# Four token tiles of the last chunk accumulated ahead of its last two steps, statistics of six tiles on ScalarE, and all blocks of u ahead of the operand differences

## The chip, the cores and the metric

The kernel runs as one program on one core of a Trainium2 chip. The metric is device time in microseconds (us) from start to end of one execution; the median of three executions is compared.

## The reference

Two blocks are computed one after the other on 1024 tokens (rows) of width 1024, in float32; the first has two layers. What the change touches are the feed-forward parts and the layer norms behind them:

```python
    # first block, each layer: mixer, then
        x = layer_norm(ALPHA * x + gate * y, ln_g[layer, 0], ln_b[layer, 0])
        u = x * (1.0 + scale) + shift
        y = jnp.square(jax.nn.relu(u @ mlp_w1[layer] + mlp_b1[layer])) @ mlp_w2[layer] + mlp_b2[layer]
        x = layer_norm(ALPHA * x + gate * y, ln_g[layer, 1], ln_b[layer, 1])
    # second block: mixer, then
        x = _layernorm(DEEPNORM_ALPHA * x + mix, ln1_g, ln1_b)
        h = _causal_depthwise_conv(x @ w_up, conv_f_w, conv_f_b)
        gate, val = h[..., :D_FF_2], h[..., D_FF_2:]
        ffn = (jax.nn.silu(gate) * val) @ w_down
        x = _layernorm(DEEPNORM_ALPHA * x + ffn, ln2_g, ln2_b)
```

There are three such parts: the MLP of layer 0 (4096 wide, some 470 to 1165 us of the span), the MLP of layer 1 (some 1978 to 2690 us) and the gated FFN of the second block (2816 wide, some 2993 us to the end).

## The kernel before

**Matmuls.** Every float32 operand is split into a high part (a cast on ScalarE, ACT) and a low part (source minus high part, a subtraction on VectorE, DVE), and every product is three TensorE (PE) matmuls: high by high, high by low, low by high. The casts and subtractions of weights are in `ws.split` (L216, L218; tiles `wl`, `wu`), those of the other operands in lines L1339 (`we`), L1446 (`he`) and L577 (`u`). GpSimd is called POOL, SyncE (which issues the loads and stores) SP. Each engine runs its instructions in the order of the program; a wait holds up all that stands behind it on that engine.

**The three stages of a feed-forward part.** `boundary` finishes the stage ahead: for each of 8 token tiles (128 rows) it accumulates the last weight blocks (`last_sums`, 12 matmuls for each half of 512 columns), adds them to the rows (`acc` or `xres`), takes mean and variance (`bn_stats`, L627), works out one over the root (`ln_fin`, a chain of small DVE instructions) and normalises on ACT (L631). Then it transposes the rows into `u` tiles (`u_tile`: 4 transposes on PE, scale and shift on ACT L576, cast on ACT L577, low part on DVE), eight for each half of the tokens, and runs the first three column blocks of the up projection (`fm_mms`, tiles `pss[0]` to `pss[2]`, two halves of some 48 matmuls each). `FmProducts` then does the up projection with seven products in the place of eight for each 2 x 2 block; its operands from `u` are differences of blocks, which `diffs` works out: eight DVE subtractions and four ACT casts into tiles `t`, four times. Its weight operands `we` come from sums of weight blocks (`sf`, `wx`, made on POOL) and are split on ACT and DVE. `TmProducts` does the down projection in chunks, seven steps j = 0 to 6 to a chunk, each with operands `he` from `rh` (loaded) and `rw` (weights and their sums); it splits the operands of the next step during a step, and adds each step's PSUM result (`ps`, or the two smaller buffers `pb`) to `acc` on DVE.

**Where the sum ends.** `second_half` runs `TmProducts` with a function `step` that is called four times in each step; in the last chunk it calls `add_residual` (load of the saved residual rows into `zi`, in an MLP a product with the gate row on POOL, then an addition on DVE) for the four quarters of `acc` and `ws.split` for the eight blocks that remain: four of `h` and four of w2, which a plain product sums at the end (`tail_blocks`, `last_sums`). The remaining splits spread over steps 0 to 6. For an MLP the next `boundary` does those last sums, for the FFN `finish`: for each token tile two halves of 12 matmuls, two additions, `bn_stats`, `rsqrt` (twelve small DVE instructions for a pair of tiles, nine for one) and `scale` (four DVE instructions of 128x512, or ACT and POOL for the halves listed in `_FIN_POOL`), then the store.

**The place of u and differences.** In `boundary` the u tiles of the second half are made during the first half's matmuls in the order of blocks 0, 4, 1, 5, 2, 6, 3, 7, and `diffs` follows every second of them:

```python
                    u_tile(xres, 1, kt, uT, G, B, uf=raw(1, kt))
                    if kt > 3 and ops is not None:
                        diffs([[raws[h, kt - 4 + 4 * a] for a in range(2)] for h in range(2)], ops)
```

Of the kernel before, what the change touches and what calls it, by code (L numbers as in the profile page):

```python
# [12 lines left out]
AF = mybir.ActivationFunctionType  # L13
# [241 lines left out]
def tile_net(ctx: ExitStack, tc: tile.TileContext, x, wts, ada, adag, cols, rows, sfm, rgw, wup, wsp, out):  # L255
# [118 lines left out]
    st = _K()  # L374
    st.direct = {}
    plan = []

# [129 lines left out]

    def last_sums(hs, wsx, t):

# [10 lines left out]
        if t == 0:  # L520
            o = [PSUM()[:, 0:512] for _ in range(2)]
            for dh in range(2):
                mms(o[dh], dh, range(n - 1))
            for dh in range(2):
                mms(o[dh], dh, [n - 1])
                yield o[dh]
        else:
            for dh in range(2):
                o = PSUM()[:, 0:512]
                mms(o, dh, range(n))  # L530
                yield o
# [38 lines left out]
    def u_tile(xz, h, kt, uT, G, B, lo=None, uf=None):  # L570
# [7 lines left out]
        tt(uT[h][:, 1, kt, :], uf, uT[h][:, 0, kt, :].bitcast(F32), SUB, lo)  # L578

    def boundary(hs, wsx, xres, G, B, keys, evacs, spill=None, ops=None):  # L580

# [26 lines left out]
        raws = {}  # L608
        for t in range(8):
            s6 = smt(12, "s6").rearrange("p (a b) -> p a b", b=6)  # L610
            if t == 5:
                alloc_u(uT, 0)
            sums = last_sums(hs, wsx, t)
            for dh in range(2):
                if t >= 5:
                    for _ in range({(5, 0): 2, (6, 0): 2}.get((t, dh), 1)):
# [6 lines left out]
                if t == 0 and dh == 0:  # L623
# [12 lines left out]
            else:  # L636
                z()
            if t == 1 and spill is not None:
                rr[0], rr[1] = T4("gr"), T4("cr")
                xrows(*spill[1:], rr[0], rr[1])  # L640
            if t in (2, 4, 6):
                ws.split(ws.ng + t // 2, lo=pool)
        pss = [PSUM() for _ in range(3)]
# [731 lines left out]
    class TmProducts:  # L1375
# [89 lines left out]

        def run(self, xres, step):
            aa = None
            for g in range(self.n):
# [8 lines left out]
                for t in range(4):  # L1477
# [98 lines left out]
    class Mlp:  # L1576
# [20 lines left out]
        def run(self, uT, jobs=None):  # L1597
# [47 lines left out]
            undefer(9)  # L1645
            return second_half(l, tp, 2 * l + 1, residual_job(ALPHA, f"lng{2 * l}", f"lnb{2 * l}", (f"b2_{l}", 2 * l + 1)))

# [20 lines left out]

    def second_half(l, tp, gate, job):

# [21 lines left out]
        def step(g, t):  # L1692
# [9 lines left out]
        tp.run(xres, step)  # L1702
        add_residual(xres, gate, 1, 0)
        hs, w2 = tail_blocks()
        return hs, w2, xres

# [588 lines left out]
    def ffn(bargs):  # L2295
# [68 lines left out]
        undefer(9)  # L2364
        return second_half(2, tp, None, residual_job(ALPHA2, "ln1g", "ln1b", None))

    def finish(hs, wsx, xres):
# [22 lines left out]
        for t in range(8):  # L2390
# [3 lines left out]
            s6 = smt(12, "s6").rearrange("p (a b) -> p a b", b=6)  # L2394
            for dh, o in enumerate(last_sums(hs, wsx, t)):
                f = slice(dh * 512, (dh + 1) * 512)
                tt(xres[:, t, f], xres[:, t, f], o, ADD)
                dve.bn_stats(out=s6[:, dh, :], in_=xres[:, t, f])
            dve.bn_aggr(out=mv[:, len(group) - 1, :], in_=s6)
            if later and t < 7:  # L2400
# [6 lines left out]
            if t == 6:  # L2407
                scale(*later.pop(0))
        for g in later:
            scale(*g)  # L2410


    with tc.manual_schedule():
# [25 lines left out]
        xres, w2 = st.xres, tail_end()  # L2439
        hs, w2, xres = ffn((w2[4:8], w2[0:4], xres, C("ln1g", 0, 8), C("ln1b", 0, 8), [("up", 0), ("up", 22), ("up", 1)]))  # L2440
        finish(hs, w2, xres)

# [18 lines left out]
```

## Time and profile before

| | us |
|---|---|
| median of three executions | 3713.23 (3707.98 to 3713.67) |
| the profiled execution | 3706.28 |
| its span (first to last instruction) | 3704.4 |
| PE busy | 3515.9, 95% of the span |
| DVE busy | 2663.2, 72% |
| ACT busy | 1469.9, 40% |
| POOL busy | 568.2, 15% |

The profile is of one execution. Its groups of instructions give a count, the mean duration of one and the idle time of the engine ahead of them with what ended it; its timeline gives start and duration of every instruction; its stretches give busy times, the granted clock of PE (PEclk; 1.00 is 2.4 GHz, 0.50 is 1.2 GHz) and DMA. PE is busy for 95% of the span, so that nearly all that can be won or lost lies in the few stretches where PE stands.

### The profile page before, as it was taken

The numbers are of one execution on the slowest core, as the hardware profiler recorded it, in microseconds if no ns is written. First come the engines' busy times: TensorE is split into PE (matmuls) and PEld (weight loads), VectorE is DVE, ScalarE is ACT, GpSimd is POOL, SyncE is SP. The second block draws the span as 40 slices with busy tenths as digits, with TensorE's granted clock in tenths as the row PEclk, the third lists the DMA queues.
The fourth block names the chain that finished last, engine by engine and source line by source line (L and its number), as shares of the span: only waits on it lengthen the run. The fifth ranks groups of instructions, "written<-read, shape, count | busy, mean of one in ns | idle before, by whom it ended". The sixth has DMA issues, their size and how long they took to land. (4 is left out here: it accounts for less than half of the span.)

```text
span 3704.4 us, 43629 instructions
## 1 busy us (share of the span) xinstructions
PE 3515.9 (95%) x17098; PEld 2864.4 (77%) x17098; DVE 2663.2 (72%) x3640; ACT 1469.9 (40%) x1957; POOL 568.2 (15%) x415
## 2 busy tenths in 40 slices
PE   7999899999999999999899999999989999999997
PEld 5877778887877778888787888877768677777765
DVE  5574767868997764454647666798889677877897
ACT  4254353343335442443425334432413354444431
POOL 2002113300022000000202331002200013322002
PEclk9999999999999999999999999999989999999998
DMA  6343235465642222100122445574210323222662
GB/s 228 109 135 122 80 129 190 174 229 199 238 132 93 71 81 81 46 30 30 67 93 104 149 148 213 190 264 137 100 54 29 125 76 110 88 87 104 222 218 91
DMA packets 184160, 469.16 MB, mean 127 GB/s; under 512 B 15601, under 2 KB 20353, under 8 KB 183954
## 3 DMA queue, kind: packets, MB, share of 16 engines
q1 hardware_dynamic: 177378, 446.35, 34.1%
q0 software_dynamic: 6576, 20.03, 1.6%
q8 instruction: 134, 2.20, 0.2%
q14 instruction: 72, 0.59, 0.0%
HBM read 340.99 MB, written 125.32 MB: 126 GB/s over the span
## 5 line engine op out<-in xcount | busy, mean ns | idle before, releaser
L247 PE MATMUL ps<-u,wu 128*128 128x512 f32 x2880 | 755.6, 408 | 13.9 <-ACT u L577 5.3
L247 PEld LDWEIGHTS ps<-u,wu 128*128 128x128 f32 x2880 | 533.0, 192 | 140.1 <-issue 14.0
L247 PE MATMUL ps<-he 128*128 128x512 f32 x2442 | 582.9, 397 | 28.0 <-DVE he L305 21.7
L247 PEld LDWEIGHTS ps<-he 128*128 128x128 f32 x2442 | 460.6, 190 | 144.6 <-DVE he L305 33.0
L247 PE MATMUL ps<-t,we 128*128 128x512 f32 x1728 | 423.5, 393 | 5.4 <-DVE cc L305 5.3
L247 PEld LDWEIGHTS ps<-t,we 128*128 128x128 f32 x1728 | 323.4, 188 | 83.3 <-DVE cc L305 8.8
L247 PE MATMUL pb<-u,we 128*128 128x512 f32 x1152 | 281.9, 393 | 0.0
L247 PE MATMUL ps<-wu,u 128*128 128x256 f32 x1920 | 262.5, 291 | 16.4 <-DVE wu L218 14.3
L247 PEld LDWEIGHTS ps<-wu,u 128*128 128x128 f32 x1920 | 243.0, 193 | 27.4 <-DVE wu L218 15.1
L247 PEld LDWEIGHTS pb<-u,we 128*128 128x128 f32 x1152 | 216.2, 188 | 49.5 <-DVE we L305 0.2
L1446 ACT CAST he<-rw 128x1024 fp32r<-128x1024 f32 (+1 forms) x154 | 132.7, 911 | 240.4 <-DVE rw L305 227.0
L247 PE MATMUL ps<-pw,wu 128*128 128x512 f32 x816 | 211.3, 407 | 14.5 <-DVE xres L308 8.8
L1925 DVE TENSOR_REDUCE mx<-ps 128x1 f32<-128x128 f32 (+7 forms) x128 | 95.6, 755 | 173.5 <-PE ps L247 173.1
L305 DVE TENSOR_TENSOR we<-sf,we 128x512 fp32r<-128x512 f32 x192 | 153.9, 814 | 85.7 <-ACT we L1339 84.7
L305 DVE TENSOR_TENSOR he<-rw,he 128x1024 fp32r<-128x1024 f32 (+1 forms) x154 | 162.6, 1098 | 61.4 <-ACT he L1446 61.2
L1965 ACT ACTIVATE p<-ps 128x1024 f32<-128x1024 f32 (+7 forms) x128 | 82.9, 649 | 304.2 <-PE ps L247 288.4
L247 PEld LDWEIGHTS ps<-pw,wu 128*128 128x128 f32 x816 | 155.0, 194 | 51.5 <-DVE xres L308 9.2
L305 DVE TENSOR_TENSOR he<-rh,he 128x1024 fp32r<-128x1024 f32 (+1 forms) x154 | 165.9, 1079 | 18.6 <-ACT he L1446 18.4
L1446 ACT CAST he<-rh 128x1024 fp32r<-128x1024 f32 (+1 forms) x154 | 136.5, 911 | 88.5 <-DMA rh<-d_h 81.7
L305 DVE TENSOR_TENSOR acc<-acc,ps 128x1024 f32<-128x1024 f32 (+1 forms) x148 | 154.1, 1042 | 17.0 <-PE ps L247 16.6
L305 DVE TENSOR_TENSOR we<-wx,we 128x512 fp32r<-128x512 f32 x144 | 134.3, 934 | 44.5 <-ACT we L1339 44.5
L247 PE MATMUL pb<-he 128*128 128x512 f32 x666 | 158.5, 392 | 0.0
(395 smaller groups left out, 5847.7 us busy)
## 6 DMA issues: line engine op xcount, KB each, us to landing
st<-in_wts_dram SPq DMA_DIRECT2D x108, 512.0 KB, 3.4
rh<-d_h SPq DMA_DIRECT2D x105, 512.0 KB, 5.4
sf<-in_wts_dram SPq DMA_DIRECT2D x96, 512.0 KB, 6.6
d_h<-hx SPq DMA_DIRECT2D x37, 1024.0 KB, 5.1
d_h<-rr SPq DMA_DIRECT2D x111, 256.0 KB, 2.3
sta<-in_ada_dram SPq DMA_DIRECT2D x48, 512.0 KB, 3.6
rw<-in_wts_dram SPq DMA_DIRECT2D x28, 768.0 KB, 6.1
sta<-in_adag_dram SPq DMA_DIRECT2D x32, 512.0 KB, 3.9
```

The lines of the kernel that those rows point to most:

```text
L247: return self.eng.matmul(out=out, lhsT=lhsT, rhs=rhs, **kw)
L305: (eng or dve).tensor_tensor(out=o, in0=a, in1=b, op=op)
L1446: act.copy(d[:, 0, 0:n, :], src)
L1925: dve.tensor_reduce(out=mx[:, t:t + 1], in_=ps[:, 0:n], axis=AX.X, op=ALU.max)
L1965: act.activation(out=p[:, 128 * i:1024], in_=ps[:, 128 * i:1024], func=AF.Exp)
```

## The change

Three things are changed.

1. **Early tiles.** After step j = 4 of the last chunk a new function `mid` is called: it adds the quarter (0,1) of the residual, splits the last two weight blocks (`tail_blocks`) and accumulates and normalises token tiles 0 to 3 (`early_tiles` in an MLP, the first half of `finish`, now a generator, in the FFN), with the small PSUM buffers `pb` (two of them) in the place of `ps` (three). Steps 5 and 6 follow. `boundary` then begins at tile 4 and makes one u tile in each half of tiles 4 to 7.
2. **Statistics.** In `finish` the mean and variance of tiles 0 to 5 come from two ACT instructions with an accumulated output (Copy, then Square with the negative mean as bias), with one small DVE instruction between them; tiles 6 and 7 keep `bn_stats`.
3. **u ahead of differences.** The four calls of `diffs` come after all eight u tiles of the second half: the first within the second half of `pss[0]`, the second behind it, the third behind the first evacuation, the fourth behind the matmuls of `pss[2]`.

```diff
+    def early_tiles(hs, wsx, xres):
+        for t in range(4):
+            s6 = smt(12, "s6").rearrange("p (a b) -> p a b", b=6)
+            for dh, o in enumerate(last_sums(hs, wsx, t, True)):
+                xr = xres[:, t, dh * 512:(dh + 1) * 512]
+                tt(xr, xr, o, ADD)
+                dve.bn_stats(out=s6[:, dh, :], in_=xr)
+            y, nb = ln_fin(s6)
+            act.activation(out=xres[:, t, :], in_=xres[:, t, :], func=AF.Identity, scale=y, bias=nb)
+        st.first = 4
...
-                    if kt > 3 and ops is not None:
-                        diffs([[raws[h, kt - 4 + 4 * a] for a in range(2)] for h in range(2)], ops)
+        def diff(j):
+            if ops is not None:
+                diffs([[raws[h, j + 4 * a] for a in range(2)] for h in range(2)], ops)
+
         for c, _ in enumerate(fm_mms(pss[0], w[0], uT, 1)):
             if c % 2:
                 residual(4 + c // 2)
+            if c == 3:
+                diff(0)
+        diff(1)
         ws.split(ws.ng + 1, True, lo=pool)
         run(fm_mms(pss[1], w[1], uT, 1))
         evacs[0](pss[0])
+        diff(2)
         run(fm_mms(pss[2], w[2], uT, 1))
+        diff(3)
         evacs[1](pss[1])
...
+                if g == self.n - 3:
+                    mid()
...
             if g >= tp.n - 7:
-                if t == 3 and j in (2, 5, 6):
-                    add_residual(xres, gate, *((0, 0), (0, 1), (1, 1))[(2, 5, 6).index(j)])
-                ws.split(min(ws.ng + 8, max(ws.ns, ws.ng + (4 * j + t) // 3)))
+                if (j, t) == (2, 3):
+                    add_residual(xres, gate, 0, 0)
+                elif (j, t) == (6, 0):
+                    add_residual(xres, gate, 1, 1)
+                if j < 5:
+                    ws.split(min(ws.ng + 8, max(ws.ns, ws.ng + (4 * j + t) // 3)))
...
+        def mid():
+            add_residual(xres, gate, 0, 1)
+            r.extend(tail_blocks())
+            early(*r, xres)
+        tp.run(xres, step, mid)
         add_residual(xres, gate, 1, 0)
...
+            else:
+                xr, dev = xres[:, t, :], T4("dev")
+                act.activation(out=dev, in_=xr, func=AF.Copy, scale=1.0 / 1024, accum_out=m[:, 0:1])
+                nm = smt(1, "nm")
+                ts(nm, m[:, 0:1], -1.0 / 32, None, MUL)
+                act.activation(out=dev, in_=xr, func=AF.Square, bias=nm, scale=1.0 / 32, accum_out=m[:, 1:2])
```

DVE's queue in the boundary of layer 0's MLP, before, from the low part of the second pair of u tiles on (`tx`, `ur`, `t`: a set of differences):

```order
L305 TENSOR_TENSOR u_3557<-ur,u_3557 128x512
L305 TENSOR_TENSOR u_3559<-ur,u_3559 128x512
L305 TENSOR_TENSOR tx<-ur 128x512
L305 TENSOR_TENSOR tx<-ur,tx 128x512
L305 TENSOR_TENSOR ur<-ur,tx 128x512
L305 TENSOR_TENSOR ur<-ur 128x512
L305 TENSOR_TENSOR t_3637<-tx,t_3637 128x512 x2
L305 TENSOR_TENSOR t_3638<-ur,t_3638 128x512 x2
L305 TENSOR_TENSOR u_3558<-ur,u_3558 128x512
L305 TENSOR_TENSOR u_3560<-ur,u_3560 128x512
```

And after, on the same engine from the third u tile on:

```order
L305 TENSOR_TENSOR u_3557<-ur,u_3557 128x512
L305 TENSOR_TENSOR u_3559<-ur,u_3559 128x512
L305 TENSOR_TENSOR u_3558<-ur,u_3558 128x512
L305 TENSOR_TENSOR u_3560<-ur,u_3560 128x512
L305 TENSOR_TENSOR u_3558<-ur,u_3558 128x512
L305 TENSOR_TENSOR u_3560<-ur,u_3560 128x512
L305 TENSOR_TENSOR tx<-ur 128x512
L305 TENSOR_TENSOR tx<-ur,tx 128x512
L305 TENSOR_TENSOR ur<-ur,tx 128x512
L305 TENSOR_TENSOR ur<-ur 128x512
L305 TENSOR_TENSOR t_3689<-tx,t_3689 128x512 x2
L305 TENSOR_TENSOR t_3690<-ur,t_3690 128x512 x2
```

The u tiles stand in a row now, and the four sets of differences in a row behind them.

DVE's queue in the last chunk of the FFN, before, from the sum of weights for step 6 on (`rw`); `acc<-acc,pb` is the result of step 4:

```order
L305 TENSOR_TENSOR rw<-rw 128x1536
L305 TENSOR_TENSOR acc<-acc,pb 128x512
L305 TENSOR_TENSOR he<-rw,he 128x1024
L305 TENSOR_TENSOR he<-rw,he 128x512
L305 TENSOR_TENSOR he<-rh,he 128x1024
L305 TENSOR_TENSOR acc<-acc,ps 128x2x512
L218 TENSOR_TENSOR wl<-st,wl 128x1024
L305 TENSOR_TENSOR he<-rh,he 128x512
L305 TENSOR_TENSOR acc<-acc,ps 128x2x512
L305 TENSOR_TENSOR acc<-acc,zi 128x2x512 x2
L218 TENSOR_TENSOR wl<-st,wl 128x1024
```

And after; behind these rows come the rest of tiles 0 to 3 (a `rsqrt` for tiles 0 and 1, the additions of tiles 2 and 3, the `scale` of tile 1, a `rsqrt` for tiles 2 and 3), and only then the four rows of `he`:

```order
L305 TENSOR_TENSOR rw<-rw 128x1536
L305 TENSOR_TENSOR acc<-acc,pb 128x512
L305 TENSOR_TENSOR acc<-acc,zi 128x2x512 x2
L218 TENSOR_TENSOR wl<-st,wl 128x1024 x2
L305 TENSOR_TENSOR acc<-acc,pb 128x512 x2
L312 TENSOR_SCALAR nm<-mvp 128x1
L305 TENSOR_TENSOR acc<-acc,pb 128x512 x2
L312 TENSOR_SCALAR nm<-mvp 128x1
```

The additions of `zi` and the last two splits of w2 stand right behind step 4's result, ahead of the additions of tile 0, and the operands `he` of step 6 stand behind all of tiles 0 to 3. The same holds in the two MLPs.

SP's queue at the end of the program, a piece of the difference:

```order
-L1524 DMA zi<-d_zm 128x2x512 x6
-L2387 DMA out_dram<-acc 128x512 x16
-L2457 UNCONDITIONAL_BRANCH
+L1548 DMA zi<-d_zm 128x2x512 x2
+L2424 DMA out_dram<-acc 128x512 x4
+L1548 DMA zi<-d_zm 128x2x512 x4
+L2424 DMA out_dram<-acc 128x512 x12
+L2506 UNCONDITIONAL_BRANCH
```

The stores of tiles 0 and 1 stand ahead of the last four loads of the residual.

## Rows read from the trace of the kernel before

**Rows 1.** Stretches: us, each engine's busy time (instructions), PEclk, DMA share, GB/s.

```profile
480.00:497.00 17.00, 12.64 (x46) 9.57 (x47) 14.58 (x24) 11.84 (x19) 0.00 (x0) 0.80 0.28 93
1049.90:1165.00 115.10, 102.81 (x461) 81.18 (x460) 95.35 (x169) 43.07 (x54) 32.36 (x20) 0.99 0.24 82
2563.40:2690.00 126.60, 118.58 (x536) 95.77 (x536) 113.13 (x199) 47.75 (x58) 40.28 (x18) 0.99 0.30 104
```

**Rows 2.** Who PE waited for, 470 to 525 us: total us, times, longest.

```profile
PE pb L251 <- ACT ur L576: 4.8, 2, 2.4
PE ps L247 <- ACT u L577: 1.7, 1, 1.7
```

**Rows 3.** DVE's instructions in order of time, 473 to 517 us: start, us.

```profile
475.36 0.69 DVE L305 TENSOR_TENSOR tx<-ur 128x512 f32<-128x512 f32 x1
...
480.63 0.69 DVE L305 TENSOR_TENSOR u<-ur,u 128x512 fp32r<-128x512 f32 x1
481.96 0.69 DVE L305 TENSOR_TENSOR u<-ur,u 128x512 fp32r<-128x512 f32 x1 [0.64 <-ACT u L577]
...
513.24 0.69 DVE L305 TENSOR_TENSOR we<-sf,we 128x512 fp32r<-128x512 f32 x1 [2.36 <-ACT we L1339]
```

**Rows 4.** All engines in order of time, 504 to 530 us.

```profile
501.93 2.47 POOL L218 TENSOR_TENSOR wu<-st,wu 128x1024 fp32r<-128x1024 f32 x1 [41.47 <-ACT wu L216]
...
521.21 2.96 PE L247 MATMUL ps<-u,we 128*128 128x512 f32 x12
```

**Rows 5.** All engines in order of time, 3025 to 3050 us.

```profile
3026.18 2.60 DVE L308 SCALAR_TENSOR_TENSOR rr<-ps,col,rr 128x1023 f32<-128x1023 f32 x2 [0.86 <-ACT rr L2304]
...
3044.45 2.92 PE L247 MATMUL ps<-u,we 128*128 128x512 f32 x12
```

**Rows 6.** All engines in order of time, 1045 to 1072 us.

```profile
1049.90 11.11 PE L247 MATMUL ps<-he 128*128 128x512 f32 x48
...
1053.91 0.68 DVE L305 TENSOR_TENSOR acc<-acc,pb 128x512 f32<-128x512 f32 x1
...
1054.67 2.42 POOL L305 TENSOR_TENSOR acc<-acc,gate 128x1024 f32<-128x1024 f32 x1 [3.96 <-DVE acc L305]
...
1061.65 3.28 POOL L305 TENSOR_TENSOR acc<-acc,gate 128x1024 f32<-128x1024 f32 x1 [4.57 <-DVE acc L305]
...
1062.63 3.39 DVE L305 TENSOR_TENSOR he<-rh,he 128x1024 fp32r<-128x1024 f32 x1
```

**Rows 7.** DMA issues of the whole span: KB each, median us to landing.

```profile
zi<-d_zm SPq DMA_DIRECT2D x24, 512.0 KB, 4.4
```

**Rows 8.** PE in order of time, 2595 to 2605 us.

```profile
2600.02 5.32 PE L247 MATMUL ps<-wl,wu 128*128 128x512 f32 x15 [3.93 <-DVE acc L305]
```

**Rows 9.** All engines in order of time, 2556 to 2584 us.

```profile
2561.54 2.38 DVE L218 TENSOR_TENSOR wl<-st,wl 128x1024 fp32r<-128x1024 f32 x1
...
2563.45 13.08 PE L247 MATMUL ps<-he 128*128 128x512 f32 x56
```

**Rows 10.** All engines in order of time, 3612 to 3640 us.

```profile
3615.88 16.77 PE L247 MATMUL ps<-he 128*128 128x512 f32 x72
...
3617.42 0.68 DVE L305 TENSOR_TENSOR acc<-acc,pb 128x512 f32<-128x512 f32 x1
...
3625.54 2.36 DVE L305 TENSOR_TENSOR acc<-acc,zi 128x1024 f32<-128x1024 f32 x2
```

**Rows 11.** DVE's and ACT's instructions in order of time, 3664 to 3704 us.

```profile
3685.68 0.15 DVE L314 TENSOR_SCALAR lnv<-mvp 128x1 f32<-128x1 f32 x1
...
3690.13 0.74 DVE L308 SCALAR_TENSOR_TENSOR acc<-acc,mvp,orow 128x512 f32<-128x512 f32 x1
...
3693.02 0.21 DVE L314 TENSOR_SCALAR nb<-mvp,lny 128x1 f32<-128x1 f32 x1
```

**Rows 12.** ACT's groups of instructions by line and shape: busy us, mean ns.

```profile
L631 ACT ACTIVATE acc<-acc,nb,lny 128x1024 f32<-128x1024 f32 x16 | 19.9, 1243 | 78.7 <-DVE nb L314 78.7
...
L1081 ACT ACTIVATION_READ_ACCUMULATOR wk<-pb 128x1 f32 x32 | 6.6, 207 | 0.0
```

More of the change, by code (lines that the diff above doesn't have):

```diff
@@ L375, in tile_net @@
     st.direct = {}
+    st.first = 0
     plan = []
@@ L506, in tile_mms, with last_sums @@
         return ps
-    def last_sums(hs, wsx, t):
+    def last_sums(hs, wsx, t, small=False):
         n = len(hs)
@@ L520, in last_sums @@
         if t == 0:
-            o = [PSUM()[:, 0:512] for _ in range(2)]
+            o = [PB() if small else PSUM()[:, 0:512] for _ in range(2)]
             for dh in range(2):
@@ L528, in last_sums @@
             for dh in range(2):
-                o = PSUM()[:, 0:512]
+                o = PB() if small else PSUM()[:, 0:512]
                 mms(o, dh, range(n))
@@ L608, in boundary @@
         raws = {}
-        for t in range(8):
+        first, st.first = st.first, 0
+        ut = 4 if first else 5
+        for t in range(first, 8):
             s6 = smt(12, "s6").rearrange("p (a b) -> p a b", b=6)
-            if t == 5:
+            if t == ut:
                 alloc_u(uT, 0)
@@ L614, in boundary @@
             for dh in range(2):
-                if t >= 5:
-                    for _ in range({(5, 0): 2, (6, 0): 2}.get((t, dh), 1)):
+                if t >= ut:
+                    for _ in range(1 if first else {(5, 0): 2, (6, 0): 2}.get((t, dh), 1)):
                         kt = todo.pop(0)
@@ L622, in boundary @@
                 o = next(sums)
-                if t == 0 and dh == 0:
+                if t == first and dh == 0:
                     flush()
@@ L637, in boundary @@
                 z()
-            if t == 1 and spill is not None:
+            if t == (4 if first else 1) and spill is not None:
                 rr[0], rr[1] = T4("gr"), T4("cr")
                 xrows(*spill[1:], rr[0], rr[1])
-            if t in (2, 4, 6):
-                ws.split(ws.ng + t // 2, lo=pool)
+            if t in ((4, 5, 6) if first else (2, 4, 6)):
+                ws.split(ws.ng + (t - 3 if first else t // 2), lo=pool)
         pss = [PSUM() for _ in range(3)]
@@ L1464, in fetch, with run @@
                 self.weights(c + 1, *((0, 0), (1, 0), (0, 1), (1, 1))[j - 2])
-        def run(self, xres, step):
+        def run(self, xres, step, mid):
             aa = None
@@ L1645, in run @@
             undefer(9)
-            return second_half(l, tp, 2 * l + 1, residual_job(ALPHA, f"lng{2 * l}", f"lnb{2 * l}", (f"b2_{l}", 2 * l + 1)))
+            return second_half(l, tp, 2 * l + 1, residual_job(ALPHA, f"lng{2 * l}", f"lnb{2 * l}", (f"b2_{l}", 2 * l + 1)), early_tiles)
     def begin(tp, i):
@@ L1667, in begin, with second_half @@
             tp.sums(2)
-    def second_half(l, tp, gate, job):
+    def second_half(l, tp, gate, job, early):
         xres = Rows("acc")
@@ L1696, in step @@
             if g >= tp.n - 7:
-                if t == 3 and j in (2, 5, 6):
-                    add_residual(xres, gate, *((0, 0), (0, 1), (1, 1))[(2, 5, 6).index(j)])
-                ws.split(min(ws.ng + 8, max(ws.ns, ws.ng + (4 * j + t) // 3)))
+                if (j, t) == (2, 3):
[4 more added lines that the diff above has]
+                    ws.split(min(ws.ng + 8, max(ws.ns, ws.ng + (4 * j + t) // 3)))
             elif g == tp.n - 8 and t == 3:
                 run(side_work)
-        tp.run(xres, step)
+        r = []
+        def mid():
[3 more added lines that the diff above has]
+        tp.run(xres, step, mid)
         add_residual(xres, gate, 1, 0)
-        hs, w2 = tail_blocks()
-        return hs, w2, xres
+        return r[0], r[1], xres
     def zip_cost(a, b, rate, at_end):
@@ L2364, in ffn, with early_out @@
         undefer(9)
-        return second_half(2, tp, None, residual_job(ALPHA2, "ln1g", "ln1b", None))
+        return second_half(2, tp, None, residual_job(ALPHA2, "ln1g", "ln1b", None), early_out)
+    def early_out(hs, wsx, xres):
+        st.fin = finish(hs, wsx, xres)
+        next(st.fin)
     def finish(hs, wsx, xres):
@@ L2394, in finish @@
             s6 = smt(12, "s6").rearrange("p (a b) -> p a b", b=6)
-            for dh, o in enumerate(last_sums(hs, wsx, t)):
+            m = mv[:, len(group) - 1, :]
+            for dh, o in enumerate(last_sums(hs, wsx, t, t < 4)):
                 f = slice(dh * 512, (dh + 1) * 512)
                 tt(xres[:, t, f], xres[:, t, f], o, ADD)
-                dve.bn_stats(out=s6[:, dh, :], in_=xres[:, t, f])
-            dve.bn_aggr(out=mv[:, len(group) - 1, :], in_=s6)
+                if t > 5:
+                    dve.bn_stats(out=s6[:, dh, :], in_=xres[:, t, f])
+            if t > 5:
+                dve.bn_aggr(out=m, in_=s6)
+            else:
[4 more added lines that the diff above has]
+                act.activation(out=dev, in_=xr, func=AF.Square, bias=nm, scale=1.0 / 32, accum_out=m[:, 1:2])
             if later and t < 7:
@@ L2408, in finish @@
                 scale(*later.pop(0))
+            if t == 3:
+                yield
         for g in later:
@@ L2439, in tile_net @@
         xres, w2 = st.xres, tail_end()
-        hs, w2, xres = ffn((w2[4:8], w2[0:4], xres, C("ln1g", 0, 8), C("ln1b", 0, 8), [("up", 0), ("up", 22), ("up", 1)]))
-        finish(hs, w2, xres)
+        ffn((w2[4:8], w2[0:4], xres, C("ln1g", 0, 8), C("ln1b", 0, 8), [("up", 0), ("up", 22), ("up", 1)]))
+        run(st.fin)
 def kernel(**inputs):
```

## The prediction

> **What bounds the kernel now.** The page says that PE is busy for 95% of the span, so I looked for the stretches that the change touches and, in each, for the time in which PE stands. The stretches come first [rows 1]: in the boundary ahead of layer 0's first product (480 to 497 us) PE is busy for 12.64 of 17.0 us at a granted clock of 0.80; at the end of layer 0's MLP and in the boundary behind it PE idles 115.1 - 102.8 = 12.3 us, in layer 1's 126.6 - 118.6 = 8.0 us, and there DVE is busy for 113 of 126.6 us. So DVE, with PE's clock behind it, is what these boundaries wait for. The second view is who PE waited for [rows 2]: 4.8 + 1.7 us for ACT's parts of u tiles. The third is time order, for what DVE and POOL do at the places of change [rows 3 to 6, 9 to 11]. The sum is made against the profiled execution's 3706.3 us, which lies 6.9 us under the median of 3713.2.
>
> **u ahead of differences (three boundaries).** A set of differences takes DVE 480.63 - 475.36 = 5.3 us, 5.2 without the gap, and the low parts of u wait behind it [rows 3]; that is PE's wait of 6.5 us. Beside it stands the lower clock: at 0.80 over 17 us, some 6.8 us at 1.2 GHz, of which PE worked three quarters and lost half, 2.5 us. Both go: 9.0 us for each boundary, the same pattern standing at all three. What comes late next is the first product's weights `we`, which stand behind all differences on DVE. In an MLP: from 475.4 six more u tiles at the pace of 1.33 us (481.96 - 480.63) end at 483.4; four sets of differences, 20.8, end at 504.2. POOL has its split of 2.47 us [rows 4] and three sums of weights in the same time, together some 6.4 us (the sums taken at half of its split). DVE's two-operand instructions stand still while POOL runs one: an operand of 1.2 us took 3.39 beside a POOL product of 3.28 [rows 6]. So 510.6; four subtractions of `hx` at 0.69, 513.4; casts and splits of `we`, some 2.5, 516. PE would be there at 521.2 - 9.0 = 512.2 [rows 4], and waits 4; behind a wait of 3.9 us PE was seen to take 5.32 us for 15 matmuls [rows 8] that take 3.5 at the pace of 72 in 16.77 [rows 10], so 1.9 us more at the lower clock. Gain 9.0 - 4 - 1.9 = **3 us in each MLP**. In the FFN three convolutions stand in DVE's queue as well, 3 x 2.6 us and a product of 1.2 [rows 5], with no `hx`: by the same walk 3007 + 20.8 + 6.4 + 9.0 + 2 = 3045, against PE at 3044.45 - 9.0 = 3035.4. The wait is 9.8 + 1.9, a **loss of 2.7 us**. Before, the covers were 8 us from `we` (513.24) to PE's use (521.21): the change spends them. Bounds: 9 gained in each if POOL holds nothing up, 3 lost in each if more is held up. Sum taken: -3.3 us.
>
> **Early tiles in layer 0's MLP.** PE reaches tile 0 at 1049.9 [rows 6]. Six matmuls (1.4 us) use the first two w2 blocks; then it needs the third, whose low part now stands on DVE behind the last result of step 4 (1053.91 + 0.68), and two additions of `zi`, which wait for POOL's gate product (1054.67 + 2.42 = 1057.1) [rows 6]. Two additions at 1.2 and one split at 1.2 make 1060.7: PE waits 9 us from 1051.3, and 1.9 us go at the lower clock. Two PSUM buffers in the place of three cost about 1 us more (each half has 2.8 us of PE work, its addition 0.7). What was waiting for that work before, 12.3 us of idle time and perhaps 1 of clock, does not all go: the u tiles and the normalisations of tiles 4 to 7 stay in order. I take half, 6 + 1. Loss 12 - 7 = **5 us** (bounds: all of it goes, 0; none goes, 12). Steps 5 and 6 cover the normalisations of tiles 0 to 3; that is the gain in that half.
>
> **The same in layer 1.** Here the two loads of `zi` share a buffer in the row of the temporaries: the first can issue when the split at 2561.54 is done (2563.9) [rows 9], lands 4.4 us later [rows 7] and is added at 2569.5; the second takes its place, lands at 2573.9 and is added at 2575.1; the split makes 2576.3. PE, at tile 0 from 2563.45 [rows 9], waits from 2564.9: 11.4 us, 1.9 at the lower clock, 1 for the buffers, 14.3 together. Against it half of 8.0 and the 1.9 behind the wait of 3.93 [rows 8]: **loss 8.5 us** (bounds 4 and 15).
>
> **The end.** PE reaches tile 0 at 3615.9, needs the third block at 3617.3 and gets it at 3617.4 + 0.7 + 2.4 + 1.2 = 3621.7 [rows 10]: 4.4 us, 1.9 of clock, 1 of buffers. The other 90 matmuls (21.0) end at 3645.6, step 5 (36 matmuls, 8.4) at 3654. Step 6's operands `he` now stand on DVE behind tiles 0 to 3: last addition 3646.3, ACT's Copy with its accumulator (no such row; by the normalisation's 1.24 and an accumulator read's 0.21 [rows 12], 1.45; bounds 1.0 and 2.0), `scale` of tile 1 (4 x 0.75 [rows 11]), a `rsqrt` of 12 small instructions at 0.15 to 0.21 each [rows 11], 2.4, and three splits of 0.6 to 1.2: 3656.4. PE waits 2.4 us, loses some 1 of clock, ends step 6 at 3665.8 and the second half of tile 5 at 3677.0. From there DVE leads: addition 0.7, Copy 1.45 and the negative mean, `scale` of tile 3 (3), `rsqrt` (2.4): 3685.0; tile 6's additions and `bn_stats`, 3.0; `rsqrt`, 2 to 4.45 (beside POOL 3685.68 to 3690.13 [rows 11]); tile 7's, 3.0; `rsqrt`, 2 to 4.45; `scale` of tile 6, 2.9. The last `nb`, at 3693.02 before [rows 11], comes at 3698 to 3703, and what follows it is unchanged. The statistics moved to ACT take four times 0.7 us off DVE for tiles 4 and 5, but put DVE behind ACT's Copy for 1.45 us a tile. SP's four stores ahead of the last `zi` loads cost nothing: those additions stand behind step 6's operands at 3656. **Loss 7.4 us** (5 to 10).
>
> **Sum.** -3.3 + 5 + 8.5 + 7.4 = 17.6 us slower, 3723.9 against the profiled execution, **3731 us** against the median.
>
> **The rivals.**
>
> *POOL does not hold DVE up at the new places.* Then the MLPs' weights come by 509.6, ahead of PE's 512.2, and each boundary keeps its 9 us; the FFN waits 3.4 + 1.9 and keeps 3.7; the last stretch loses 5, the other two 4 and 8.5: -21.7 + 17.5 = -4.2 us, 3709 us, not slower. It decides at `we`'s readiness before 512.2. Against it stands the operand that took 3.39 in the place of 1.2 us [rows 6]; for it, that POOL may have run its instructions in the u tiles' time, where DVE has gaps of 0.64 us [rows 3]. The Trainium skill (Advanced Engine Details and Errata, VectorE Performance Modes) says that GpSimd and two-port VectorE instructions block each other, and lists no two-port mode for a tensor_tensor; by that rule alone this rival holds, and the trace speaks against it.
>
> *DVE's total decides in the boundaries.* With 113 of 126.6 us busy, PE's wait at tile 0 is only one that it would have had later. Both boundaries come out even, 17.6 - 13.5 = 4.1 us slower, 3717. It decides where DVE's idle time does not grow; against it, DVE itself stands for two loads and POOL's product.
>
> *Both together:* -17.7 us, 3695.
>
> *All at the bad bounds:* 3 lost at each `we`, 9 and 13 in the boundaries, 10 at the end, 9 + 22 + 10 = 41, 3754.
>
> **How the numbers follow.** The forecast has 0.50, the first rival 0.15, the second 0.15, both 0.10, the last 0.10. Of the forecast some lies either side of its 3731 by the halves taken, 3722 to 3742. A measurement of this kernel tells 0.2%, 7.4 us, from no change: faster is under 3705.8, same up to 3720.7. Faster: both rivals together and a third of the first, with part of the halves taken too large, 0.17; same: the rest of the first and nearly all of the second, 0.23; slower: 0.60. The range of 3700 to 3745 leaves out most of the case of both and most of the last, under 2 in 10.
>
> **What would show it.** In the profile after, PE's waits for u should be gone from 480 to 497 us, and a wait for `we` of about 4 us (MLPs) and 10 us (FFN) should stand ahead of the first product; PE should wait 9, 11 and 4 us for `wl` early in tile 0; a wait for `he` should stand ahead of step 6 of the last chunk; and the last `nb` should be reached by way of DVE, not PE. The forecast is wrong if `we` is ready ahead of PE, if the loads of `zi` have landed early so that the splits follow step 4 at once, or if the waits of tiles 4 to 7 vanish altogether.

## The result, and the profile after

| | before | changed |
|---|---|---|
| median, us | 3710.61 (3707.92 to 3713.67, 4 runs) | 3733.14 (3728.49 to 3733.74, 4 runs) |
| ratio to before | | 1.0053, 95% interval 1.004 to 1.0065 |
| span of the profiled execution | 3704.4 | 3726.7 |
| PE busy | 3515.9 | 3518.9 |

The change makes the kernel 0.53% slower, some 22 us; 3731 was forecast. PE does the same work (17098 matmuls in both traces): what is new is waiting, and the lower clock behind it. To see where, the same matmul (by its count from the start; the count stands in the same place of the program outside the reordered stretches) is looked up in both traces. The table gives by how much it starts later in the trace after:

| stretch | on entry | on leaving | change | forecast |
|---|---|---|---|---|
| u and first product, layer 0 (470 to 530 us) | +0.1 | -5.2 | -5.3 | -3 |
| end of layer 0's MLP, boundary (1040 to 1170) | -4.3 | +0.4 | +4.7 | +5 |
| u and first product, layer 1 (1978 to 2040) | +1.5 | -3.9 | -5.4 | -3 |
| end of layer 1's MLP, boundary (2540 to 2692) | -4.9 | +5.1 | +10.0 | +8.5 |
| u and first product, FFN (2990 to 3055) | +4.8 | +5.7 | +0.9 | +2.7 |
| FFN's last steps to the end (3590 on) | +7.9 | +22.3 | +14.4 | +7.4 |

The rest, 3 us, is drift between the stretches. The sum of the six rows is 19.3 us where 17.6 were forecast, so the sum came out well; but the first part won more than forecast, 9.8 us in place of 3.3, and the end lost about twice as much. The last row even hides some of that loss: 2.6 us are won between 3590 us and the place where tile 0 begins (3615.9 before, 3621.2 after, +5.3), in steps that the change leaves as they were. From tile 0 on, which is what the forecast of 7.4 is about, the loss is 17.0 us.

**Ahead of the first products.** Who PE waited for in the trace after, 470 to 530 us and 2985 to 3065 us (total us, times, longest):

```profile
PE ps L247 <- ACT we L1361: 3.4, 1, 3.4
...
PE ps L247 <- ACT we L1361: 9.2, 1, 9.2
```

The waits for u [rows 2] are gone, and those for `we` stand in their place, 4 and 9.8 us in the forecast. The trace after in order of time, 484 to 520 us, shows who held `we` up:

```profile
494.71 2.45 POOL L218 TENSOR_TENSOR wu<-st,wu 128x1024 fp32r<-128x1024 f32 x1 [34.10 <-ACT wu L216]
494.82 2.89 DVE L305 TENSOR_TENSOR tx<-ur 128x512 f32<-128x512 f32 x1
...
499.68 1.62 POOL L305 TENSOR_TENSOR wx<-wx,sf 128x512 f32<-128x512 f32 x1
500.07 1.77 DVE L305 TENSOR_TENSOR ur<-ur 128x512 f32<-128x512 f32 x1
...
508.13 1.15 ACT L1296 CAST t<-ur 128x512 fp32r<-128x512 f32 x2 [0.78 <-DVE ur L305]
...
513.37 0.60 ACT L1361 CAST we<-sf 128x512 fp32r<-128x512 f32 x1
...
514.03 4.79 PE L247 MATMUL ps<-u,we 128*128 128x512 f32 x12 [3.45 <-ACT we L1361]
```

The subtraction `tx<-ur`, 0.69 us in [rows 3], takes 2.89 while POOL's split takes 2.45, and `ur<-ur` 1.77 beside POOL's sum. The first product comes at 514.03 where it came at 521.21 [rows 4], and its 12 matmuls take 4.79 us in place of 2.96: from 516 to 519 us the granted clock is 0.50. PE's wait itself ends with ACT's cast of `we` at 513.37. On ACT that cast stands behind the four instructions that evacuate two finished blocks (509.17 to 513.5), and these behind the casts of the last set of differences, which waited for DVE. So DVE's queue reaches `we` by way of ACT's, and not by way of DVE's `hx` as the prediction had it.

**Early tiles.** Who PE waited for longest in the trace after, 1036 to 1070, 2550 to 2590 and 3605 to 3680 us:

```profile
PE pb L247 <- DVE wl L218: 8.6, 2, 7.6
...
PE pb L247 <- DVE wl L218: 11.4, 1, 11.4
...
PE pb L247 <- DVE wl L218: 8.0, 1, 8.0
PE ps L247 <- DVE acc L305: 4.0, 1, 4.0
```

9, 11.4 and 4.4 us were forecast for the first three, 2.4 for the fourth. The trace after in order of time shows what holds the split up: at the end of layer 0's MLP (first row) POOL's gate product, at the end of layer 1's the two loads that share a buffer, one landing after the other (the time in brackets is DVE's idle time and what ended it):

```profile
1053.71 1.23 DVE L305 TENSOR_TENSOR acc<-acc,zi 128x1024 f32<-128x1024 f32 x1 [2.23 <-POOL acc L305]
...
2562.74 2.43 DVE L305 TENSOR_TENSOR acc<-acc,zi 128x1024 f32<-128x1024 f32 x1 [1.07 <-DMA zi<-d_zm]
...
2568.95 1.23 DVE L305 TENSOR_TENSOR acc<-acc,zi 128x1024 f32<-128x1024 f32 x1 [3.79 <-DMA zi<-d_zm]
2570.09 2.35 DVE L218 TENSOR_TENSOR wl<-st,wl 128x1024 fp32r<-128x1024 f32 x2
...
2571.37 5.06 PE L247 MATMUL pb<-wl,wu 128*128 128x512 f32 x11 [11.43 <-DVE wl L218]
```

And the last chunk of the FFN, in order of time:

```profile
3628.71 1.23 DVE L305 TENSOR_TENSOR acc<-acc,zi 128x1024 f32<-128x1024 f32 x1 [3.20 <-DMA zi<-d_zm]
3629.85 2.35 DVE L218 TENSOR_TENSOR wl<-st,wl 128x1024 fp32r<-128x1024 f32 x2
3631.12 17.64 PE L247 MATMUL pb<-wl,wu 128*128 128x512 f32 x65 [8.00 <-DVE wl L218]
...
3665.22 1.22 DVE L305 TENSOR_TENSOR he<-rh,he 128x1024 fp32r<-128x1024 f32 x1
3666.35 1.21 DVE L305 TENSOR_TENSOR acc<-acc,ps 128x1024 f32<-128x1024 f32 x1
...
3667.71 10.94 PE L247 MATMUL ps<-he 128*128 128x512 f32 x36 [4.01 <-DVE acc L305]
...
3715.31 0.21 DVE L314 TENSOR_SCALAR nb<-mvp,lny 128x1 f32<-128x1 f32 x1
```

Here DVE, done with the first addition of `zi`, stands 3.20 us for the second load; the split follows, and PE stands for 8.0 us. Step 6's 36 matmuls begin behind a wait of 4.0: its operand splits, and the addition of step 5 that frees its PSUM buffer, stand on DVE behind tiles 0 to 3. They then take 10.94 us at the pace that gave 8.4 [rows 10]. The last `nb` comes at 3715.31 where it came at 3693.02 [rows 11], 22.3 us later, as the whole.

### The profile page after: what moved, and what is told of

It is laid out like the page before. It is cut to its first block, busy times and chain, and to the rows that moved or that the text cites. A ratio compares the mean times of both kernels' runs of the same rounds, so it can differ in the third digit from the quotient of the medians.

```text
span 3726.7 us, 43662 instructions
## 1 busy us (share of the span) xinstructions
PE 3518.9 (94%) x17098; PEld 2866.5 (77%) x17098; DVE 2670.4 (72%) x3628; ACT 1486.0 (40%) x1981; POOL 571.0 (15%) x415
## 5 line engine op out<-in xcount | busy, mean ns | idle before, releaser
L247 PE MATMUL ps<-u,we 128*128 128x512 f32 x576 | 146.2, 403 | 16.0 <-ACT we L1361 15.9
```

The costliest lines, as they stand in the source:

```text
L247: return self.eng.matmul(out=out, lhsT=lhsT, rhs=rhs, **kw)
```

## The experiments

The theory: each part costs what PE waits at its own place, by the order in DVE's queue; POOL's products add to that queue where DVE leads. The first rival: POOL does not hold DVE up. The second: DVE's total decides, and a wait taken away only moves. Each run's ratio is to the kernel before, run beside it on the same chip.

**The third part alone.** The kernel before with this edit only:

```diff
-                    if kt > 3 and ops is not None:
-                        diffs([[raws[h, kt - 4 + 4 * a] for a in range(2)] for h in range(2)], ops)
+        def diff(j):
+            if ops is not None:
+                diffs([[raws[h, j + 4 * a] for a in range(2)] for h in range(2)], ops)
...
+            if c == 3:
+                diff(0)
+        diff(1)
...
+        diff(2)
...
+        diff(3)
```

> The kernel before with the third part of the change alone: the differences behind all u tiles, in all three boundaries; no early tiles, no statistics on ScalarE. Theory (each part costs what it costs at its own place): the trace after puts the first products 5.3 and 5.5 us earlier in the two MLPs and 0.9 us later in the FFN, so 10 us faster than before, about 3701 us, with PE waiting some 3.4 us for we in the MLPs and 9 in the FFN. Rival (what is won ahead of the first product is given back in the products behind it, which are paced by DVE and POOL): within 2 us of before, 3709 to 3713.

Measured: 3704.41 us against 3713.03, ratio 0.9979 (0.997 to 0.9989): 8.6 us faster. This part of the change is a gain, and most of it is kept behind the first products; in the trace of this run 1.5 and 2.6 us are given back at the ends of the two MLPs.

**Without the early tiles of the FFN.** The changed kernel, the FFN's last chunk and `finish` as before:

```diff
-        return second_half(2, tp, None, residual_job(ALPHA2, "ln1g", "ln1b", None), early_out)
+        return second_half(2, tp, None, residual_job(ALPHA2, "ln1g", "ln1b", None), None)
...
-        tp.run(xres, step, mid)
+        tp.run(xres, step, mid if early else (lambda: None))
```

> The changed kernel with the last chunk of the FFN and finish as before: no early tiles and no statistics on ScalarE at the end of the program, the rest as changed. Theory: the last stretch (3590 us to the end) lost 14.4 us in the trace after, all of it by the early tiles there; so 3733 - 14 = 3719 us. Rival (the end is bound by the same DVE work whichever way it is ordered, and the loss came from a late arrival): 3729 to 3733.

Measured: 3715.86 us against 3713.03, ratio 1.001 (1.0 to 1.002). The theory holds. With the run above this divides the 22 us: the third part -8 to -9, the early tiles of the MLPs +11, those of the FFN with the statistics +16 to 17 (1.0053 against 1.001, and 17.0 by the count of matmuls from tile 0 on).

**The statistics.** Twice, once in the changed kernel and once alone. The changed kernel with `bn_stats` for all tiles:

```diff
-                if t > 5:
+                if True:
                     dve.bn_stats(out=s6[:, dh, :], in_=xres[:, t, f])
-            if t > 5:
+            if True:
                 dve.bn_aggr(out=m, in_=s6)
```

> The changed kernel with the statistics of all tiles on DVE as before, everything else as changed. Theory: tiles 0 to 3 have room on DVE; for tiles 4 and 5 DVE takes 1.4 + 0.2 us and gives up the wait of 1.3 us for ACT's Copy: within 2 us of the changed kernel, 3731 to 3735. Rival (the statistics on ScalarE cost the end its time): 4 to 8 us faster, 3725 to 3729.

Measured: 3728.2 us against 3714.06, ratio 1.0033 (1.002 to 1.0047), against 1.0053 (1.004 to 1.0065) with the statistics on ACT. And the differences behind u, with the ACT statistics for tiles 0 to 5 and no early tiles:

```diff
-                dve.bn_stats(out=s6[:, dh, :], in_=xres[:, t, f])
-            dve.bn_aggr(out=mv[:, len(group) - 1, :], in_=s6)
+                if t > 5:
+                    dve.bn_stats(out=s6[:, dh, :], in_=xres[:, t, f])
+            if t > 5:
+                dve.bn_aggr(out=m, in_=s6)
+            else:
+                xr, dev = xres[:, t, :], T4("dev")
+                act.activation(out=dev, in_=xr, func=AF.Copy, scale=1.0 / 1024, accum_out=m[:, 0:1])
...
```

> The kernel with the differences behind the u tiles (3704), and of the second part the statistics alone: tiles 0 to 5 of the end get mean and variance from ScalarE, all tiles after step 6 as before. Theory (the end's loss is the order, not the statistics): DVE gives up six times 1.6 us and stands six times some 1.3 us for ACT's Copy, so 0 to 2 us faster, 3702 to 3704. Rival (DVE behind ACT's mean is what makes the end slower): 5 to 8 us slower, 3709 to 3712.

Measured: 3709.48 us against 3714.06, ratio 0.9985 (0.9976 to 0.9994), where the same without the statistics had 0.9979. In both the theory missed: they point the same way, to 2 to 7 us lost by the statistics, but in both the intervals touch. The count of matmuls settles the sign. From the matmul that begins tile 0 in the changed kernel to the last one, each by its count, the third part alone loses 0.1 us on the kernel before, and with the ACT statistics 4.0; the changed kernel loses 17.0, and with `bn_stats` 10.9. Part of that last step is chance, since PE waited 5.5 us for `wl` in that run and not 8.0, ahead of all statistics; a further run of the changed end with a wait of 5.5 (the changed kernel with POOL's work on DVE, below) loses 14.2. So like against like the statistics lose 3.2 and 4.0 us; of five other traces with the end as before four lie within 0.1 us of the kernel before and one at 1.0. What they lose it by is seen in DVE behind ACT; the trace of the second run at the end, DVE in order of time:

```profile
3668.98 0.15 DVE L312 TENSOR_SCALAR nm<-mvp 128x1 f32<-128x1 f32 x1 [1.90 <-ACT dev L2413]
3669.05 1.46 DVE L308 SCALAR_TENSOR_TENSOR acc<-acc,mvp,orow 128x512 f32<-128x512 f32 x1
```

For a product on one column, 0.15 us, DVE stands 1.90 us here and 1.2 to 1.3 us in the other eleven tiles of the two traces, while `scale` of a tile that is ready can wait behind it.

**The split ahead of zi.** The changed kernel with two lines exchanged:

```diff
         def mid():
-            add_residual(xres, gate, 0, 1)
             r.extend(tail_blocks())
+            add_residual(xres, gate, 0, 1)
             early(*r, xres)
```

> The changed kernel with the last two splits of w2 ahead of the quarter (0,1) of the residual, so that the split's low parts no longer stand behind the loads of zi and POOL's product. Theory (PE's waits at tile 0 are those for the split, and behind them for zi): the waits for wl of 7.6, 11.4 and 8.0 us fall to about 1; the additions of tile 0 now stand behind zi, and with two PSUM buffers PE waits for the third half instead, some 4, 6 and 4 us. About 12 us faster than the changed kernel, 3721. Rival (DVE's total decides, PE's wait only moves): within 3 us of 3733.

Measured: 3727.66 us against 3713.03, ratio 1.0043 (1.0028 to 1.0058): some 4 to 5 us faster than the changed kernel, with intervals that touch, and not 12. Who PE waited for in this run, 1036 to 1070 and 2550 to 2590 us:

```profile
PE pb L247 <- DVE wl L218: 4.0, 2, 3.0
PE pb L247 <- DVE acc L305: 3.5, 1, 3.5
...
PE pb L247 <- DVE acc L305: 8.4, 1, 8.4
PE pb L247 <- DVE wl L218: 2.8, 1, 2.8
```

In layer 1 the wait of 11.4 us for `wl` became 2.8 for it and 8.4 for the addition of tile 0, which stands behind `zi`: 11.2 together. In layer 0 8.6 became 7.5. By the count of matmuls nothing is won in the MLPs (6.0 and 10.2 us lost, 4.7 and 10.0 in the trace after): the wait is for `zi` there, whichever of the two stands first. In the FFN, where no gate product is due, the wait for `wl` falls to 2.2 us with 0.8 for an addition, and from tile 0 to the end 11.1 us are lost in place of 14 to 17. So DVE's order decides in the FFN, and in the MLPs step 4 is too early for the tiles in either order.

**The tiles one step later.** The changed kernel with tiles 0 to 3 after step 5:

```diff
-                if g == self.n - 3:
+                if g == self.n - 2:
                     mid()
...
+                elif (j, t) == (4, 3):
+                    add_residual(xres, gate, 0, 1)
...
-                if j < 5:
-                    ws.split(min(ws.ng + 8, max(ws.ns, ws.ng + (4 * j + t) // 3)))
+                if j < 6:
+                    ws.split(min(ws.ng + 8, max(ws.ns, ws.ng + (4 * j + t + 1) // 3)))
...
         def mid():
-            add_residual(xres, gate, 0, 1)
             r.extend(tail_blocks())
```

> The changed kernel with tiles 0 to 3 after step 5 instead of after step 4: the quarter (0,1) of the residual is loaded at the end of step 4, the last two splits go through step 5 and step 6's operands stand ahead of the tiles on DVE. One step of 8 to 11 us remains behind the tiles instead of two. Theory (the loss is the waiting for zi, the splits and step 6's operands): the waits of 7.6, 11.4 and 8.0 us for wl and of 4.0 us for he go with the clock lost behind them (about 6 + 2.5), some of it taken back by less cover; 20 to 30 us faster than the changed kernel, 3703 to 3713. Rival (DVE's total decides): 3725 to 3733.

Measured: 3710.62 us against 3713.03, ratio 0.9998 (0.9989 to 1.0007): by the ratios 20 us of the 22 are back. In the same stretches PE still waited 3.6, 5.1 and 0.5 us for `wl`; so next the splits were put ahead by three calls more:

```diff
-                    ws.split(min(ws.ng + 8, max(ws.ns, ws.ng + (4 * j + t + 1) // 3)))
+                    ws.split(min(ws.ng + 8, max(ws.ns, ws.ng + (4 * j + t + 4) // 3)))
```

> As the run with tiles 0 to 3 after step 5, with all eight weight blocks split one step's quarter earlier each, the last at the end of step 4 (DVE then does the last two splits ahead of step 4's last additions and of zi). Theory: the waits for wl that were left there (3.6, 5.1 and 0.5 us) go, with about 3 us of clock behind them: 8 to 12 us faster than that run's 3711, about 3701. Rival (in that variant the early tiles cost what DVE's other work needs, and PE's wait moves on to the additions): 3708 to 3713.

Measured: 3707.12 us against 3714.06, ratio 0.9976 (0.9967 to 0.9986), 8 us faster by the ratios. No wait for `wl` is left in the three stretches; 1.2, 1.4 and 0.9 us for the PSUM buffers `pb` are. By the count of matmuls the two MLP ends, which lost 4.7 and 10.0 us in the trace after, now gain 5.8 and 4.0, and the end loses 4.7, about what the statistics lose alone. The rival of DVE's total falls here: with the same work on DVE, the order alone is worth some 28 us.

**POOL's work on DVE.** The run with the third part alone, and in its boundaries the split behind the second set of differences and the three sums of the first product's weights on DVE:

```diff
-        ws.split(ws.ng + 1, True, lo=pool)
+        ws.split(ws.ng + 1, True)
         run(fm_mms(pss[1], w[1], uT, 1))
...
-                tt(x[:, 0:512], a21, a22, ADD, pool)
-                tt(x[:, 512:1024], x[:, 0:512], a11, SUB, pool)
-                tt(a21, a11, a21, SUB, pool)
+                e_ = pool if q else None
+                tt(x[:, 0:512], a21, a22, ADD, e_)
+                tt(x[:, 512:1024], x[:, 0:512], a11, SUB, e_)
+                tt(a21, a11, a21, SUB, e_)
```

> The kernel with the differences behind the u tiles (3704), with POOL's work in those boundaries given to DVE: the low part of the weight split behind the second set of differences, and the three sums of the first product's weights. Theory (a POOL product holds DVE up for its whole time, and takes longer for it): DVE gives up some 7 us of standing beside POOL and takes on 1.2 + 3 x 0.7 = 3.3 us, so the first product starts up to 3.5 us earlier in each of the three: 8 to 12 us faster with the clock, 3693 to 3697. Rival (POOL runs beside DVE and its rows are only long because it waits itself): DVE's queue grows by 3.3 us in each, 3712 to 3716.

Measured: 3686.05 us against 3714.06, ratio 0.9924 (0.991 to 0.9939): 28 us faster than before, 20 us by the ratios over the third part alone, twice what was expected. The trace of this run, in order of time from 490 us:

```profile
495.65 1.21 DVE L218 TENSOR_TENSOR wu<-st,wu 128x1024 fp32r<-128x1024 f32 x1
...
496.79 0.68 DVE L305 TENSOR_TENSOR tx<-ur 128x512 f32<-128x512 f32 x1
...
511.25 0.63 PE L247 MATMUL ps<-u,we 128*128 128x512 f32 x2
```

The same `tx<-ur` takes 0.68 us and not 2.89, and DVE does the split in 1.21 us for which POOL took 2.45. By the count of matmuls the three first products start 3.7, 3.7 and 3.1 us sooner against the run with the third part alone: 10.5 us, as expected. The spans differ by 3704.0 - 3683.7 = 20.3 us; the other 10 lie in other stretches: 4.5 between 1210 and 1240 us, at the start of layer 1's mixer, 1.5 and 2.7 at the ends of the two MLPs, the rest in smaller steps. That all of these come from the edit isn't shown.

The same edit on the changed kernel and on the kernel before:

> The changed kernel with POOL's work of the boundaries (the split behind the second set of differences, the first product's weight sums) on DVE, nothing else. Theory (the prediction's walk of the first part: what holds we back there is DVE standing beside POOL): PE's waits of 3.4, 3.3 and 9.2 us ahead of the first products fall by 3 to 3.5 each and the whole gains what the same edit gained on the differences alone, 18 us: 3715, still not faster than before, since the early tiles' waits stay. Rival (the early tiles take up what DVE gains): 3725 or more.

Measured: 3713.28 us against 3711.92, ratio 1.0002 (0.9989 to 1.0015). PE's waits for `we` fell from 3.4, 3.3 and 9.2 us to 1.4, 1.3 and 6.1, and 19 us were won in all by the ratios; those at tile 0 stay at 7.6 and 11.6 in the MLPs, and the one in the FFN is 5.5 where it was 8.0.

> The kernel before with the same POOL work on DVE and nothing else changed, the differences still between the u tiles. Theory (the edit pays where DVE leads): PE still waits for u ahead of the first products, and we had 8 us to spare there, so nothing is won at those three places; only the boundaries without differences gain, together some 8 us: 3706. Rival (the edit gains by itself, whatever the order of u): 18 us faster, 3696.

Measured: 3713.54 us against 3711.92, ratio 0.9998 (0.9986 to 1.0009). Alone it wins nothing, not even the 8 us expected of the other boundaries. The two edits pay together: with the differences between the u tiles PE waits for u, and a shorter queue on DVE has 8 us of slack to fall into. Nor did the other boundaries gain. The stretch from 1210 to 1240 us gains 2.8 us by the edit in the changed kernel and 1.3 in the kernel before, against the 4.5 above, so part of the second 10 us of the run at 3686 comes back in other kernels; where the rest comes from stays open.

**More of it.** On top of the run at 3686, three more kinds of POOL's products on DVE:

```diff
-                tt(xr, xr, rr[1], ADD, None if t % 2 else pool)
+                tt(xr, xr, rr[1], ADD)
...
-                ws.split(ws.ng + t // 2, lo=pool)
+                ws.split(ws.ng + t // 2)
...
-                tt(x, x, gate_row[gate][:, f].unsqueeze(1).to_broadcast([128, 2, 512]), MUL, pool)
+                tt(x, x, gate_row[gate][:, f].unsqueeze(1).to_broadcast([128, 2, 512]), MUL)
```

> The run with POOL's work of the three boundaries on DVE (3686), and three more of POOL's products on DVE: the low parts of the other weight splits in the boundaries, the additions of the residual rows there, and the products with the gate row in the last chunk of each MLP. Theory (where DVE leads, a POOL product takes DVE's time for its whole length, twice what DVE itself needs): POOL's 32 and 40 us in the two MLP ends fall away and DVE takes on half of them; 5 to 10 us faster, 3676 to 3681. Rival (DVE is full there, and only what stood ahead of a first product was on the path): 3686 or up to 8 us slower.

Measured: 3700.16 us against 3714.29, ratio 0.9967 (0.9954 to 0.9981), 16 us slower than without by the ratios. The rival's direction holds, at twice the loss that it allowed for. That these products had stood in DVE's pauses is its reading; as the three kinds were moved together, the run doesn't show it for each. In the boundary ahead of layer 1's MLP PE waits anew; who PE waited for in this run, 1890 to 1965 us, where there was no wait before:

```profile
PE pb L251 <- ACT xres L631: 2.5, 1, 2.5
```

By the count of matmuls 2.7, 4.2 and 4.2 us were lost ahead of the two MLPs and the FFN and 4.5 at the end of layer 0's MLP; 3.9 were won at the end of layer 1's, where gate products went as well.

**Early tiles on top of that.** The run at 3686 with the early tiles of the two MLPs after step 5 and all splits by step 4; the FFN and the end as before:

> The run with POOL's work of the three boundaries on DVE (3686), and the early tiles 0 to 3 in the two MLPs alone, after step 5 with all splits by the end of step 4; the FFN's last chunk and the end as before. Theory (early tiles pay where they wait for nothing): the variant after step 5 passed the first MLP's end 7 us and the second's 6 us better than the differences alone did, so about 13 us faster, 3673. Rival (those gains were the standing of DVE beside POOL, which is gone here): 3683 to 3686.

Measured: 3683.61 us against 3714.29, ratio 0.9913 (0.9897 to 0.993), against 0.9924 (0.991 to 0.9939) without: not told apart. That is the rival's number, but its reason is borne out in part only: by the count of matmuls the early tiles win 3.7 and 3.6 us at the ends of the two MLPs, some half of what they won there without the POOL edit, and the first of these is lost again between 1200 and 1400 us, far from the edit. Why isn't known. Both are the fastest versions here, 0.8 to 0.9% under the kernel before.

## Why the prediction was right, point by point

**The sign and the size** were right: 3731 forecast, 3733 measured, and by the mechanisms named. The prediction's list of what should show is there: no waits for u, waits for `we` of 3.4 and 9.2 (4 and 9.8 forecast), for `wl` of 7.6, 11.4 and 8.0 (9, 11.4 and 4.4), a wait ahead of step 6, the last `nb` by way of DVE.

**u ahead of differences** was sized too small. The forecast of 3 us each took 9.0 as gain; the same matmul at 510 us lies 11.0 us further ahead than at 470, and 5.3 us are kept in layer 0, 5.4 in layer 1. The mis-sized term is the gain that the waits for u and the lower clock had cost, 11 us in place of 9.0; what was lost behind that, 4 + 1.9 in the forecast, measured 3.4 and, by difference, 2.3. In the FFN, too, 10.9 us were gained in place of 9.0, and the loss was 0.9 and not 2.7. The walk by POOL's share, 6.4 us in DVE's queue, holds: with POOL's work on DVE, which takes 3.3 us of DVE's own there, the first products come 3.1 to 3.7 us sooner, together 6.4 to 7.0.

**The early tiles of the MLPs** came as walked: 4.7 and 10.0 us against 5 and 8.5. The halves that were taken for what goes of the former waits were guesses, and together they came out 1 us off. In layer 0 even the two sides fit: by 1060 us the trace after has lost 12.1 us against tile 0's place (12 forecast), and by 1170 it has 7.3 of them back (7).

**The end** was sized at less than half: from tile 0 on 17.0 us measured, 7.4 forecast. Three terms failed. The wait for `wl` was taken as 4.4 with both loads of `zi` landed, and 1.9 of clock; the second load landed late, PE stood 8.0 us (5.5 in two other runs), and the 65 matmuls behind it took 2.5 us more than at the pace of [rows 10]: 4.2 us too little. The wait ahead of step 6 was 4.0 us with 2.5 of clock, where 2.4 and 1 were taken, 3.1 too little: the walk left out the addition of step 5's first half, 1.21 us, which stands behind the operand splits in the same queue and which PE waited for. So PE, counted from tile 0, is done with tile 5 7.4 us later than in the walk, and from there DVE leads to the end, as forecast; its own pieces beside POOL (`scale` of tile 3, 4.3 us in place of 3, and a `rsqrt` of 3.8 and one of 4.5, of which the middle of 2 and 4.45 was taken) bring the rest, 2.2. The ACT statistics, held for about neutral, are within these: taken alone they lose 3 to 4 us. Why the second load landed late isn't settled. It took 8.2 us to land in the trace after, 5.0 to 5.8 in three variants whose loads of the final scaling's rows follow it about as closely, so some 3 us of it look like chance of that execution.

**The rivals.** That POOL does not hold DVE up is refuted three times: by the rows above, by the 10 us at the first products, and by the same move in the changed kernel, whose waits for `we` shrank by 2.0, 2.0 and 3.1 us. That DVE's total decides is refuted by the variants after step 5, and held in one respect: with the split ahead of `zi` the wait in the MLPs only moved. The last case, all at the bad bounds, was summed with 9 and 13 us for the MLP ends, under the 12 and 15 that the walks name as their bounds; nothing measured hangs on it.

**The errors offset each other**, 6.5 us too little gained ahead of the first products and 9.6 too little lost at the end. The starting point helped as well: the forecast added 17.6 us to a median of 3713.2, while the kernel before took 3710.6 beside the changed one, so 22.5 us were lost. The nearness of 3731 and 3733 is partly luck.

## What to carry to other kernels

Work pulled ahead of a step also pulls ahead all that it waits for: list on every in-order engine what now stands in front of it (loads, another engine's product, a split), and what of the next step now stands behind it, before counting on the cover. Where one engine's queue leads, look at what holds that engine up: a two-input product on GpSimd cost VectorE more there than VectorE needed to do it itself, but moving three other kinds of product cost 16 us. One good part can hide in a change that loses as a whole, so time the parts.

## What the runs showed of the hardware

That DVE stands beside POOL was in the rows of before [rows 6]; new are two bounds of it. The first is what the instruction reads. DVE instructions with two SBUF inputs stand (2.89 us in place of 0.69 beside a POOL product of 2.45), those that read one input from PSUM do not: in the trace after, DVE and POOL in order of time near the end,

```profile
3688.43 5.62 POOL L305 TENSOR_TENSOR acc<-acc,orow 128x512 f32<-128x512 f32 x4 [29.12 <-ACT acc L2418]
3689.82 0.69 DVE L305 TENSOR_TENSOR acc<-acc,ps 128x512 f32<-128x512 f32 x1 [2.10 <-PE ps L247]
```

the addition from PSUM takes its 0.69 us within the second of POOL's four. In that whole trace 72 additions of 128x512 from PSUM begin while a POOL product runs, and none takes over 0.69 us. The Trainium skill (GPSIMD Engine Reference, Specifications) names contention with VectorE instructions in a two-port mode or with two SBUF inputs; the trace agrees with the second half of that (the 2.89 us); by the first half alone the first rival of the prediction would have held.

The second bound is which of the two begins first: that one runs at its own pace, and the other stands. In the rows of before [rows 6] POOL's product at 1061.65 takes 3.28 us where the one at 1054.67 takes 2.42; when it began, this split was under way:

```profile
1061.49 1.22 DVE L218 TENSOR_TENSOR wl<-st,wl 128x1024 fp32r<-128x1024 f32 x1
```

This split keeps its 1.22 us, and the operand behind it, at 1062.63, takes the 3.39. In the trace after, ten DVE splits of 128x1024 that begin ahead of a POOL product take 1.21 to 1.22 us, and thirteen that begin while one runs take 1.5 to 3.4 us.
